# 24 instead of 16 prompt tokens take their experts by gather; the gate map is made in blocks of 8 tokens and evicted a job later

## The chip, the cores and the metric

The kernel runs on one core of a Trainium2 chip. The metric is the time of one execution in microseconds on the device; of several executions the median is taken. TensorE is called PE, VectorE DVE, ScalarE ACT, GpSimd POOL and SyncE SP, as in the profile.

## The reference

One decoder layer in fp32 for 320 tokens: 256 of a prompt and 64 of a sample (8 x 8), with a model width of 2048. The part that the change touches is the expert layer:

```
def one_block(xb):                      # after q = xb wq and two top-16 searches for each of 8 heads
    e = i1 * N_KEYS + i2                # 16 experts per token and head, of 128 * 128
    g = jax.nn.softmax(sc, axis=-1)
    ue = jnp.take(u_tab, e, axis=0)
    act = jax.nn.gelu(jnp.einsum('thkd,td->thk', ue, xb))
    ve = jnp.take(v_tab, e, axis=0)
    return jnp.einsum('thk,thkd->td', g * act, ve)
```

Before it come an input projection, windowed attention, a gating unit and an output projection; behind it a gated per-layer embedding.

## The kernel before

Up to about 400 us the kernel computes projection, attention, gating unit and output projection for all 320 tokens. Then comes the expert layer, which takes two ways.

**The dense way**, for the last 240 prompt tokens (`TD`, columns `XT:TP`): all 16,384 experts are computed. There are 128 units "u" (128 experts each: their rows `uT` times the tokens, then gelu in `finish`) and 16 groups `NG` of 8 units "v" (`v_t`, which add into `hT`). A unit's 1 MB of weights is loaded by SP in `prepare(n, 0)`; for each of its two halves `prepare(n, h)` splits it into `w_hi` (ACT, L683) and `w_lo` (DVE, L684). `multiply(n, h, q)` then does 4 chunks of three products each (`mm3`, L98 to L100: high by high, high by low, low by high), 12 for each q, 24 for a half slot (n, h). Between gelu and the v units, `weights` multiplies the activations with the gate map `g_t` and splits them too.

**The gate map** says with which weight a token takes each expert. It is made before the first v unit, in `NB` = 8 tokens at a time, 30 jobs, one behind each `multiply` of the first u units. `one_hots(j)` writes on DVE e (L762) and p (L763), where the two keys of a token's choices are marked; `map_products(j)` multiplies them on PE (L775, 16 small products into two PSUM tiles, tag "s" for even jobs and "o" for odd ones, two buffers each), evicts the two tiles on ACT into the tile `g_st` (L779), and at each second job sends `g_st`, with 16 tokens, to the DRAM tensor `gd` by a DMA on POOL's queue (L786). The pool "oh" has two buffers of `g_st`, e and p. `fetch_g` reads a group's part back, for group 0 on POOL's queue, for the others on ACT's.

**The gather way**, for the first 16 prompt tokens (`XT`) and the 64 sample tokens: their experts' rows are fetched by an indirect DMA on POOL's queue into `row`, 128 rows of 2048 at a time (a `Rows` set; "c" for the sample with 64 steps, "x" for the prompt with 16), and DVE makes a dot product (L828, first pass with rows of u) or adds the weighted rows to a sum (L832, second pass with rows of v). The indices and gates of "x" come into `x_eg` by 8 small DMAs on POOL (L737). At the end PE adds the sums of the 128 rows up by token (`add_samples` for c, L875; `add_first` for x, L907), and the results go to `hT`.

The order in the dense phase is written out by hand: `tc.manual_schedule` keeps DVE, ACT and PE to the order of the program. In the loop over the first u units each slot has its `multiply` q = 0, a map job, q = 1, a map job, and then `prepare` for the next but one half; a count of microseconds (`spent`, `total`, `step_us`) spreads the gather steps over the rest.

Two lines of the schedule matter here:

```
at_ = (2 * (slot - first) + q + 1) / (2 * (2 * U1 - first))
while job < JOBS and job < round(JOBS * at_):
```

Of the kernel before, what the change touches and what calls it, by code (L numbers as in the profile page):

```python
# [10 lines left out]
F32 = mybir.dt.float32  # L11
# [28 lines left out]
WSC = 16384.0  # L40
LEAD = 32

XT = 16
TD = TP - XT
NTB = TD // 16


def build(tc, a):
# [4 lines left out]
def _build(ctx, tc, nc, a):  # L53
# [11 lines left out]
    hl = ctx.enter_context(tc.tile_pool(name="hl", bufs=4))  # L65
    ps = ctx.enter_context(tc.tile_pool(name="ps", bufs=2, space=bass.MemoryType.PSUM))
    drm = ctx.enter_context(tc.tile_pool(name="drm", bufs=1, space=bass.MemoryType.DRAM))
    gd = drm.tile([NG, P, NTB * GRP * 16], F32, name="gd")

    def psum(tag, cols, parts=P):  # L70
        t = ps.tile([P, 512], F32, tag=tag, name="ps_" + tag)
# [450 lines left out]
    i128 = load(pr, "iota", [P, NK])  # L522
    i16 = i128[:, 0:TOPK]
    stack = load(pr, "stack", [P, TS])
    stack_x = load(pr, "stack_x", [P, XT])
    c_e = pr.tile([P, 64], I32, name="c_e")
    c_g = pr.tile([P, 64], F32, name="c_g")
    x_eg = pr.tile([P, 2, TOPK], F32, name="x_eg")
    rcol = pr.tile([P, 4], F32, name="rcol")

    c_up, up = open_pool("up")
    c_rt, rt = open_pool("rt", "right")
# [5 lines left out]

    dup = rt.tile([P, 2, TS], F32, name="dup")
    vec.tensor_copy(dup, ssq[:, TP:].unsqueeze(1).to_broadcast([P, 2, TS]))  # L540
    dup_x = rt.tile([P, PH, XT], F32, name="dup_x")
    vec.tensor_copy(dup_x, ssq[:, 0:XT].unsqueeze(1).to_broadcast([P, PH, XT]))
    pm = psum("s", 512)
    pe.matmul(pm[:, 0:TP], ones_d, ssq[:, 0:TP], start=True, stop=True)
    flat = lambda d: d.rearrange("p a b -> p (a b)")
    for i, l in enumerate((ssq[:, 0:P], ssq[:, P:TP], flat(dup), flat(dup_x))):
        pe.matmul(pm[:, TP + i : TP + i + 1], l, ones_d[:, 0:1], start=True, stop=True)
    r = rstd(rt, pm[:, 0 : TP + 4], TP + 4)
    r1 = r[:, XT:TP]
    vec.tensor_copy(rcol, r[:, TP:])  # L550

# [159 lines left out]
        del sums[n], halves[n]  # L711

    NB = 8
    JOBS = NTB * 16 // NB
    oh = {}

    def key_tables():

        f = lambda i, s: R[i][:, s].rearrange("p h k -> p (h k)")
        picks = []  # L720
        for i in range(2):
            tp = psum("tr", 384)
# [12 lines left out]
        vec.tensor_copy(ex[:, 1], R[0][:XT, 2])  # L735
        for h in range(PH):
            pool.dma_start(x_eg[h * XT : h * XT + XT], ex[:, :, h])  # L737
        return picks

    def open_tables(picks):  # L740
# [24 lines left out]

    def map_products(j):
        e, parts = oh.pop(j)
        tb, hb = divmod(j, 16 // NB)
        if hb == 0:
            oh["st"] = oh["pool"].tile([P, NK, 16], F32, name="g_st")  # L770
        for q in range(NB // 4):
            gp = psum("so"[j % 2], 512)
            for t in range(4):
                for k in range(2):
                    pe.matmul(  # L775
                        gp[:, t * P : t * P + P], e[:, 1, q, :, t], parts[:, k, q, :, t], start=k == 0, stop=k == 1
                    )
            b = hb * NB + 4 * q
            act.activation(  # L779
                oh["st"][:, :, b : b + 4].rearrange("p a t -> p t a"),  # L780
                gp.rearrange("p (t a) -> p t a", t=4),
                AF.Copy,
                scale=1.0 / WSC,
            )
        if hb == 16 // NB - 1:
            pool.dma_start(  # L786
                gd[:, :, tb * P : tb * P + P].rearrange("g p x -> p g x"),
                oh["st"].rearrange("p (g i) t -> p g (i t)", g=NG),
            )

    def rows_of(dst, tmp, sl, n):

# [42 lines left out]
                vec.tensor_mul(self.w, self.w, self.g)  # L835

    def fetch_g(g, queue=nc.scalar):
        gt = vp.tile([P, NTB, GRP, 16], F32, name="g_t")
        queue.dma_start(gt.rearrange("p a b c -> p (a b c)"), gd[g])
        return gt  # L840

    def weights(g, gt):


        groups.setdefault(g, [])
        u, w = {}, {}
        for i in range(GRP + 2):
            if i >= 2:
                vec.tensor_sub(w[i - 2][1], flat4(u[i - 2]), w[i - 2][0].bitcast(F32))  # L849
                groups[g].append(w[i - 2])  # L850
            if i < GRP:
                u[i] = acts.pop(g * GRP + i)
                m = u[i].rearrange("p (a b) -> p a b", a=NTB)
                vec.tensor_mul(m, m, gt[:, :, i])
            elif i == GRP and g + 1 < NG:
                state["g"] = fetch_g(g + 1)
            if 1 <= i <= GRP:
                k = i - 1
                if k < 4 and g < NG - 1:
                    w[k] = tails[k]  # L860
                elif k < 4:
                    if k == 0:
                        state["t"] = state["xcp"].tile([P, 8, TD], F32R, tag="xc", name="thl")
# [37 lines left out]
                yield  # L901
        vec.tensor_add(ssq, total[:, 0], total[:, 1])

    def add_first():
        pt = psum("tr", NC_ * XT)
        for c in range(NC_):
            pe.matmul(pt[:, c * XT : c * XT + XT], xx[:, c * P : c * P + P], stack_x, start=True, stop=True)  # L907
            if c % 8 == 7:
                yield
        vec.tensor_add(hT[:, :, 0:XT], hT[:, :, 0:XT], pt.rearrange("p (c t) -> p c t", c=NC_))  # L910

    state = {}
    U1 = LEAD - 4
# [17 lines left out]
    with tc.manual_schedule(engines={mybir.EngineType.DVE, mybir.EngineType.Activation, mybir.EngineType.PE}):  # L931
# [2 lines left out]
                prepare(n, h)  # L934


        steps, spent, job, first = front(), 0.0, 0, None
        for n in range(U1):
            for h in range(2):
                slot = 2 * n + h  # L940
                for q in range(2):
                    multiply(n, h, q)
                    if h == 0 and q == 0 and n:
                        finish(n - 1)
                    if first:
                        at_ = (2 * (slot - first) + q + 1) / (2 * (2 * U1 - first))
                        while job < JOBS and job < round(JOBS * at_):
                            if job + 1 < JOBS:
                                one_hots(job + 1)
                            map_products(job)  # L950
                            job += 1
                if first:
                    prepare((slot + 3) // 2, 1 - h)
                else:
                    while steps and spent < 1.4 * (slot + 1):
                        cost = next(steps, None)
                        if cost is None:
                            steps = None
                        else:
                            spent += cost  # L960
                    if steps:
                        prepare(n + 2, h)
                    else:
                        first = slot + 1
        prepare(U1 + 1, 1)
        n = U1
        shut(oh["close"])
# [3 lines left out]
        for z in (A0, C):  # L971
# [2 lines left out]
        sets = [  # L974
            Rows("c", c_e, c_g, xc, rcol[:, 2:3]),
            Rows("x", x_eg[:, 0].bitcast(I32), x_eg[:, 1], xx, rcol[:, 3:4]),
        ]
        steps = [(k, j, second) for second in (False, True) for k in sets for j in range(k.n)]
        rows = {}

        def row(m):
# [4 lines left out]

        state["g"] = fetch_g(0, pool)
        to_c = rows_of(xc, state["xd"], slice(TP, T), 2)
        to_x = rows_of(xx, state["xd"], slice(0, XT), PH)
        load = weights(0, state["g"])  # L990
        for n in range(n, LEAD):
            finish(n - 1)
# [21 lines left out]
        sums_x = None  # L1014
        last_norm = last_split()
        for n in range(LEAD, len(order)):
            finish(n - 1)
# [8 lines left out]
            for h in range(2):  # L1026
# [9 lines left out]
                if m >= len(steps) - 16:  # L1036
                    next(sums_c, None)
                if sums_x:
                    next(sums_x, None)
                if order[n][0] == "v" and order[n][1] == NG - 1 and order[n][2]:  # L1040
                    next(last_norm)
                slots += 1
                while m < len(steps) and (spent + step_us / 2 < total * slots / (2 * (END - LEAD)) or n >= END):
# [2 lines left out]
                    row(m + 3)  # L1046
                    m += 1
                    spent += step_us
                if m == len(steps) and not sums_x and n >= END:
                    sums_x = add_first()  # L1050
                if n + 2 < len(order):
                    prepare(n + 2, h)
        finish(n)
# [34 lines left out]
def _constants():  # L1088
# [32 lines left out]
    stack_x = (np.arange(P)[:, None] % XT == np.arange(XT)[None, :]).astype(np.float32)  # L1121
# [88 lines left out]
```

## Time and profile before

| | us |
|---|---|
| median of 3 runs | 2134.97 |
| lowest and highest run | 2132.25, 2137.13 |
| the profiled execution | 2136.97 |
| its span | 2135.2 |

PE is busy for 98% of the span, DVE for 80%, ACT for 47% and POOL for 15%; the mean granted clock of PE is 0.993. The span is what the trace covers; an execution's own time is 1.8 us more. In the rows below an instruction's time may overlap with its neighbour's on PE, since products are pipelined: the duration of one is no measure of how many fit into a stretch.

### The profile page before, as it was taken

Reading aid. Unit: us, or ns where it says so; the run is one execution under the profiler, and the core shown is the slowest. Engines: PE = TensorE matmul, PEld = TensorE weight load, DVE = VectorE, ACT = ScalarE, POOL = GpSimd, SP = SyncE. Lnnn points to the kernel's source line nnn. Section 1 sums busy time; section 2 is a strip of 40 time slices with the busy share of each in tenths; the row PEclk is TensorE's granted clock in tenths of the full one; section 3 lists DMA queues with packets and bytes.
Section 4 is the critical chain, followed back from the end, with each engine's and each line's share of the span. In section 5 each row is a group of like instructions: output and inputs, shape, how many; then the busy total and the mean of one; then the engine's idle time right before and its main releaser. Section 6 shows DMA issues by size and latency. Waiting matters only on the chain. (4 is left out here: it accounts for less than half of the span.)

```text
span 2135.2 us, 41032 instructions
## 1 busy us (share of the span) xinstructions
PE 2101.2 (98%) x17106; PEld 2051.5 (96%) x17106; DVE 1714.6 (80%) x2563; ACT 1002.7 (47%) x1457; POOL 315.1 (15%) x231
## 2 busy tenths in 40 slices
PE   8999999999998899999999999999999999999999
PEld 7879999999998899999999999999999999999999
DVE  6574875699997768888888898898898888885754
ACT  5346554335446665444444444444444444434632
POOL 2000000000001111222222222122222222210000
PEclk9999999999999999999999999999999999999999
DMA  7312254333556688999989999999899898884452
GB/s 280 144 62 82 101 208 165 138 139 122 183 194 188 204 317 326 379 349 351 382 352 349 361 362 351 348 376 363 334 378 359 338 375 350 333 320 170 152 181 84
DMA packets 85209, 563.06 MB, mean 264 GB/s; under 512 B 9894, under 2 KB 14438, under 8 KB 22160
## 3 DMA queue, kind: packets, MB, share of 16 engines
q1 hardware_dynamic: 49936, 349.76, 44.1%
q0 software_dynamic: 29680, 191.81, 23.6%
q10 hardware_dynamic: 5408, 18.88, 2.3%
q8 instruction: 134, 2.20, 0.4%
q14 instruction: 51, 0.42, 0.1%
HBM read 541.58 MB, written 19.79 MB: 263 GB/s over the span
## 5 line engine op out<-in xcount | busy, mean ns | idle before, releaser
L683 ACT ACTIVATE w_hi<-w_raw 128x1024 fp32r<-128x1024 f32 x512 | 542.6, 1060 | 682.7 <-PE ps_o L99 362.8
L684 DVE TENSOR_TENSOR w_lo<-w_raw,w_hi 128x1024 fp32r<-128x1024 f32 x512 | 624.6, 1221 | 206.0 <-ACT w_hi L683 204.9
L98 PE MATMUL ps_mm<-a,w_hi 128*128 128x240 f32 (+1 forms) x1776 | 518.2, 292 | 2.1 <-ACT w_hi L191 1.7
L99 PE MATMUL ps_mm<-a,w_hi 128*128 128x240 f32 (+1 forms) x1776 | 518.7, 292 | 1.0 <-DVE a L123 1.0
L100 PE MATMUL ps_mm<-a,w_lo 128*128 128x240 f32 (+1 forms) x1776 | 516.6, 291 | 2.6 <-DVE w_lo L684 2.1
L98 PE MATMUL ps_mm<-c,w_hi 128*128 128x240 f32 (+1 forms) x1280 | 362.9, 283 | 0.0
L100 PE MATMUL ps_mm<-c,w_lo 128*128 128x240 f32 (+1 forms) x1280 | 361.2, 282 | 0.0
L99 PE MATMUL ps_mm<-c,w_hi 128*128 128x240 f32 (+1 forms) x1280 | 360.9, 282 | 0.0
L99 PEld LDWEIGHTS ps_mm<-a,w_hi 128*128 128x128 f32 x1776 | 336.7, 190 | 8.9 <-issue 6.6
L98 PEld LDWEIGHTS ps_mm<-a,w_hi 128*128 128x128 f32 x1776 | 336.8, 190 | 8.4 <-issue 4.8
L100 PEld LDWEIGHTS ps_mm<-a,w_lo 128*128 128x128 f32 x1776 | 336.8, 190 | 7.0 <-issue 3.2
L81 ACT ACTIVATE w_hi<-w_raw 128x1024 fp32r<-128x1024 f32 x150 | 158.6, 1059 | 282.2 <-PE ps_mm L99 188.8
L99 PE MATMUL ps_o<-wl,w_hi 128*128 128x240 f32 x1024 | 282.0, 275 | 1.1 <-DVE wl L849 1.1
L100 PE MATMUL ps_o<-wh,w_lo 128*128 128x240 f32 x1024 | 282.3, 276 | 0.0
L98 PE MATMUL ps_o<-wh,w_hi 128*128 128x240 f32 x1024 | 278.9, 272 | 0.0
L82 DVE TENSOR_TENSOR w_lo<-w_raw,w_hi 128x1024 fp32r<-128x1024 f32 x150 | 182.5, 1220 | 94.5 <-ACT w_hi L81 91.3
L100 PEld LDWEIGHTS ps_mm<-c,w_lo 128*128 128x128 f32 x1280 | 243.4, 190 | 0.2
L98 PEld LDWEIGHTS ps_mm<-c,w_hi 128*128 128x128 f32 x1280 | 243.5, 190 | 0.0
L99 PEld LDWEIGHTS ps_mm<-c,w_hi 128*128 128x128 f32 x1280 | 243.4, 190 | 0.0
L99 PEld LDWEIGHTS ps_o<-wl,w_hi 128*128 128x128 f32 x1024 | 192.7, 188 | 1.8 <-DVE wl L849 1.7
L98 PEld LDWEIGHTS ps_o<-wh,w_hi 128*128 128x128 f32 x1024 | 194.3, 190 | 0.0
L100 PEld LDWEIGHTS ps_o<-wh,w_lo 128*128 128x128 f32 x1024 | 194.3, 190 | 0.0
(382 smaller groups left out, 3792.5 us busy)
## 6 DMA issues: line engine op xcount, KB each, us to landing
w_raw<-in_uT SPq DMA_DIRECT2D x128, 1024.0 KB, 6.3
w_raw<-in_v_t SPq DMA_DIRECT2D x128, 1024.0 KB, 8.7
w_raw<-in_w_in SPq DMA_DIRECT2D x25, 1024.0 KB, 5.0
w_raw<-in_w_out SPq DMA_DIRECT2D x16, 1024.0 KB, 4.8
w_raw<-in_wq SPq DMA_DIRECT2D x16, 1024.0 KB, 4.8
w_raw<-in_w_gate SPq DMA_DIRECT2D x16, 1024.0 KB, 5.0
gd<-g_st POOLq DMA_DIRECT2D x15, 1024.0 KB, 6.5
g_t<-gd ACTq DMA_DIRECT2D x15, 960.0 KB, 8.0
```

Source lines behind the costliest of these rows:

```text
L81: last = act.activation(hi, s, AF.Copy)
L82: (lo_eng or vec).tensor_sub(lo, s, hi.bitcast(F32))
L98: pe.matmul(out, wh, xh, start=start, stop=False)
L99: pe.matmul(out, wh, xl, start=False, stop=False)
L100: pe.matmul(out, wl, xh, start=False, stop=stop)
L683: act.activation(hi, s, AF.Copy)
L684: vec.tensor_sub(lo, s, hi.bitcast(F32))
```

## The change

- `XT` is 24, so 232 columns are dense instead of 240. The 8 new tokens form a third set "y": 8 tokens x 8 heads x 2 halves of the 16 choices, 128 rows, 8 steps in each pass. Its indices and gates come by 16 small DMAs; its tokens' rows by 16 more transposes (`rows_of`), into the buffer of "c" after that set is done; a second `add_first` sums them up, now 4 products at a time.
- The sets run one after the other, each with both passes: c, x, y instead of first passes of c and x and then second ones.
- The map is stored in 29 blocks of 8 tokens: every job has its own `g_st` and its own write to `gd`.
- Eviction and write (`map_out`) of a job are issued after the products of the next job.
- In the map stretch `prepare` stands between q = 0 and q = 1, not behind both.

```diff
-XT = 16
+XT = 24
+X1 = 16
+X2 = XT - X1
 TD = TP - XT
-NTB = TD // 16
+NTB = TD // 8
...
-    JOBS = NTB * 16 // NB
+    JOBS = NTB
...
         for h in range(PH):
-            pool.dma_start(x_eg[h * XT : h * XT + XT], ex[:, :, h])
+            pool.dma_start(x_eg[h * X1 : h * X1 + X1], ex[:X1, :, h])
+
+        for i in range(2 * PH):
+            k, h = divmod(i, PH)
+            pool.dma_start(y_eg[i * X2 : i * X2 + X2], ex[X1:, :, h, k * X2 : k * X2 + X2])
...
     def map_products(j):
         e, parts = oh.pop(j)
-        tb, hb = divmod(j, 16 // NB)
-        if hb == 0:
-            oh["st"] = oh["pool"].tile([P, NK, 16], F32, name="g_st")
+        oh["out"] = []
         for q in range(NB // 4):
             gp = psum("so"[j % 2], 512)
+            oh["out"].append(gp)
...
+    def map_out(j, out):
+        st = oh["pool"].tile([P, NK, NB], F32, name="g_st")
+        for q, gp in enumerate(out):
             act.activation(
-                oh["st"][:, :, b : b + 4].rearrange("p a t -> p t a"),
+                st[:, :, 4 * q : 4 * q + 4].rearrange("p a t -> p t a"),
...
-        if hb == 16 // NB - 1:
-            pool.dma_start(
...
+        pool.dma_start(
+            gd[:, :, j * GRP * NB : (j + 1) * GRP * NB].rearrange("g p x -> p g x"),
+            st.rearrange("p (g i) t -> p g (i t)", g=NG),
+        )
...
                             map_products(job)
+                            if out:
+                                map_out(job - 1, out)
+                            out = oh["out"]
                             job += 1
-                if first:
-                    prepare((slot + 3) // 2, 1 - h)
-                else:
+                        if q == 0:
+                            prepare((slot + 3) // 2, 1 - h)
+                if not first:
...
+        map_out(JOBS - 1, out)
         prepare(U1 + 1, 1)
...
+            Rows("y", y_eg[:, 0].bitcast(I32), y_eg[:, 1], None, rcol[:, 4:5]),
         ]
-        steps = [(k, j, second) for second in (False, True) for k in sets for j in range(k.n)]
+        steps = [(k, j, second) for k in sets for second in (False, True) for j in range(k.n)]
```

On ACT, in the middle of the map stretch (L779 is the eviction and L683 the `w_hi` of the kernel before; DMASW1 and DMASW2 are the counts of POOL's DMA queue that a write to `gd` raises, PE that of the map products), there stands before:

```order
L779 ACTIVATE g_st<-ps_o 128x4x128 [waits PE_49] x2
L683 ACTIVATE w_hi<-w_raw 128x1024 [waits DVE_49]
L779 ACTIVATE g_st<-ps_s 128x4x128 [waits DMASW1_49,PE_49,Activation_49]
L779 ACTIVATE g_st<-ps_s 128x4x128 [waits PE_49]
L779 ACTIVATE g_st<-ps_o 128x4x128 [waits PE_49] x2
L779 ACTIVATE g_st<-ps_s 128x4x128 [waits DMASW2_49,PE_49,Activation_49]
```

and in the changed kernel (L792 is the eviction, L690 the `w_hi`):

```order
L792 ACTIVATE g_st<-ps_o 128x4x128 [waits DMASW1_49,PE_49,Activation_49]
L792 ACTIVATE g_st<-ps_o 128x4x128 [waits PE_49]
L690 ACTIVATE w_hi<-w_raw 128x1024 [waits DVE_49]
L792 ACTIVATE g_st<-ps_s 128x4x128 [waits DMASW2_49,PE_49,Activation_49]
L792 ACTIVATE g_st<-ps_s 128x4x128 [waits PE_49]
L792 ACTIVATE g_st<-ps_o 128x4x128 [waits DMASW3_49,PE_49,Activation_49]
```

A wait for a write stands at the eviction of each job now, where it stood at that of each second job; it is the write of the job two places back, whose `g_st` is taken again.

On POOL's queue, from the indices of the gathers to the last of them, there stands before:

```order
L737 DMA x_eg<-ex 16x2x16 x8
L786 DMA gd<-g_st 128x16x128 x15
L839 DMA g_t<-gd 128x1920
L819 DMA row<-in_u_rows,c_e 128x2048 x64
L819 DMA row<-in_u_rows,x_eg 128x2048 x16
L819 DMA row<-in_v_rows,c_e 128x2048 x64
L819 DMA row<-in_v_rows,x_eg 128x2048 x16
```

and in the changed kernel:

```order
L744 DMA x_eg<-ex 16x2x16 x8
L748 DMA y_eg<-ex 8x2x8 x16
L798 DMA gd<-g_st 128x16x64 x29
L851 DMA g_t<-gd 128x1856
L831 DMA row<-in_u_rows,c_e 128x2048 x64
L831 DMA row<-in_v_rows,c_e 128x2048 x64
L831 DMA row<-in_u_rows,x_eg 128x2048 x16
L831 DMA row<-in_v_rows,x_eg 128x2048 x16
L831 DMA row<-in_u_rows,y_eg 128x2048 x8
L831 DMA row<-in_v_rows,y_eg 128x2048 x8
```

Sixteen small DMAs stand ahead of the first write, there are 29 writes of half the size, and 16 gathers of the set y close the row.

## Rows read from the trace of the kernel before

**Rows 1.** The page: busy time of each engine, share of the span, instructions.
```profile
PE 2101.2 (98%) x17106; PEld 2051.5 (96%) x17106; DVE 1714.6 (80%) x2563; ACT 1002.7 (47%) x1457; POOL 315.1 (15%) x231
```

**Rows 2.** Four stretches; the first line names the columns.
```profile
core 0: us, PE busy (x) PEld busy (x) DVE busy (x) ACT busy (x) POOL busy (x), PEclk, DMA share, GB/s
300.00:400.00 100.00, 100.00 (x683) 99.73 (x683) 57.11 (x78) 42.20 (x60) 8.04 (x15) 1.00 0.51 179
643.00:756.00 113.00, 100.12 (x806) 96.07 (x806) 84.45 (x72) 71.95 (x79) 16.22 (x14) 0.94 0.62 188
1000.00:1100.00 100.00, 100.00 (x897) 100.00 (x896) 89.26 (x95) 44.75 (x57) 25.17 (x15) 1.00 0.92 364
```

**Rows 3.** PE by line and form: line, tiles, shapes, count | busy us, mean ns | idle.
```profile
L98 PE MATMUL ps_mm<-c,w_hi 128*128 128x240 f32 x1024 | 283.8, 277 | 0.0
...
L100 PE MATMUL ps_o<-thl,w_lo 128*128 128x240 f32 x64 | 17.5, 274 | 0.0
```

**Rows 4.** Timeline of PE at 1942 us: start us, us, engine, line, operation, tiles.
```profile
1942.41 1.85 PE L907 MATMUL ps_tr<-c_stack_x,xx 128*128 128x16 f32 x16
```

**Rows 5.** Timeline of PE at 692 us, granted clock 0.50: first and eleventh product.
```profile
691.69 0.41 PE L99 MATMUL ps_mm<-a,w_hi 128*128 128x240 f32 x1
...
693.82 0.41 PE L100 MATMUL ps_mm<-a,w_lo 128*128 128x240 f32 x1
```

**Rows 6.** Timeline of one slot of the map stretch, all engines.
```profile
697.32 2.06 PE L775 MATMUL ps_s<-p,e 128*128 128x128 f16 x16
...
698.52 1.98 ACT L779 ACTIVATE g_st<-ps_s 128x512 f32<-128x512 f32 x2 [1.26 <-PE ps_s L775]
...
700.30 1.05 ACT L683 ACTIVATE w_hi<-w_raw 128x1024 fp32r<-128x1024 f32 x1
...
700.56 2.05 PE L775 MATMUL ps_o<-p,e 128*128 128x128 f16 x16
701.39 1.23 DVE L684 TENSOR_TENSOR w_lo<-w_raw,w_hi 128x1024 fp32r<-128x1024 f32 x1 [1.79 <-ACT w_hi L683]
701.71 2.04 ACT L779 ACTIVATE g_st<-ps_o 128x512 f32<-128x512 f32 x2 [0.35 <-PE ps_o L775]
...
703.78 1.23 DVE L763 TENSOR_TENSOR p<-e,sel 128x2048 f16<-128x2048 f16 x1
...
705.06 0.28 PE L775 MATMUL ps_s<-p,e 128*128 128x128 f16 x1 [1.11 <-DVE p L763]
```

**Rows 7.** Waits of PE from 640 to 757 us: us in total, times, longest.
```profile
PE ps_o L775 <- DVE p L763: 7.0, 7, 1.3
PE ps_s L775 <- DVE p L763: 6.2, 6, 1.1
```

**Rows 8.** Map products, writes, index transfers: ns min/median/max, first and last start us.
```profile
L775 PE MATMUL ps_s<-p,e x240: 277/297/330, 643.1 to 751.2; 128*128 128x128 f16 x120
L775 PE MATMUL ps_o<-p,e x240: 285/297/330, 646.3 to 755.7; 128*128 128x128 f16 x120
...
L786 POOL DMA_DIRECT2D gd<-g_st x15: 1152/1152/1212, 649.8 to 757.5; - x15
...
DMA to landing us min/median/max: 6.0/6.5/7.5
...
L737 POOL DMA_DIRECT2D x_eg<-ex x8: 504/507/545, 637.7 to 641.6; - x8
```

**Rows 9.** DMA issues: count, KB each, median us from issue to landing.
```profile
g_t<-gd POOLq DMA_DIRECT2D x1, 960.0 KB, 4.8
...
x_eg<-ex POOLq DMA_DIRECT2D x8, 2.0 KB, 4.1
...
c_stack_x<-in_stack_x POOLq DMA_DIRECT2D x1, 8.0 KB, 2.7
```

**Rows 10.** DVE by line and form, the set x: count | busy us, mean ns | idle.
```profile
L828 DVE SCALAR_TENSOR_TENSOR row<-row,xx 128x2048 f32<-128x2048 f32 x16 | 36.5, 2282 | 0.0
L832 DVE SCALAR_TENSOR_TENSOR xx<-row,x_w,xx 128x2048 f32<-128x2048 f32 x15 | 35.2, 2346 | 0.0
```

More of the change, by code (lines that the diff above doesn't have):

```diff
@@ L67, in _build @@
     drm = ctx.enter_context(tc.tile_pool(name="drm", bufs=1, space=bass.MemoryType.DRAM))
-    gd = drm.tile([NG, P, NTB * GRP * 16], F32, name="gd")
+    gd = drm.tile([NG, P, NTB * GRP * 8], F32, name="gd")
     def psum(tag, cols, parts=P):
@@ L524, in _build @@
     stack = load(pr, "stack", [P, TS])
-    stack_x = load(pr, "stack_x", [P, XT])
+    stack_x = load(pr, "stack_x", [P, X1])
+    stack_y = pr.tile([P, X2], F32, name="stack_y")
+    vec.tensor_add(stack_y, stack_x[:, 0:X2], stack_x[:, X2:X1])
     c_e = pr.tile([P, 64], I32, name="c_e")
@@ L528, in _build @@
     x_eg = pr.tile([P, 2, TOPK], F32, name="x_eg")
-    rcol = pr.tile([P, 4], F32, name="rcol")
+    y_eg = pr.tile([P, 2, TOPK // 2], F32, name="y_eg")
+    rcol = pr.tile([P, 5], F32, name="rcol")
     c_up, up = open_pool("up")
@@ L540, in _build @@
     vec.tensor_copy(dup, ssq[:, TP:].unsqueeze(1).to_broadcast([P, 2, TS]))
-    dup_x = rt.tile([P, PH, XT], F32, name="dup_x")
-    vec.tensor_copy(dup_x, ssq[:, 0:XT].unsqueeze(1).to_broadcast([P, PH, XT]))
+    dup_x = rt.tile([P, PH, X1], F32, name="dup_x")
+    vec.tensor_copy(dup_x, ssq[:, 0:X1].unsqueeze(1).to_broadcast([P, PH, X1]))
+    dup_y = rt.tile([P, 2 * PH, X2], F32, name="dup_y")
+    vec.tensor_copy(dup_y, ssq[:, X1:XT].unsqueeze(1).to_broadcast([P, 2 * PH, X2]))
     pm = psum("s", 512)
@@ L545, in _build @@
     flat = lambda d: d.rearrange("p a b -> p (a b)")
-    for i, l in enumerate((ssq[:, 0:P], ssq[:, P:TP], flat(dup), flat(dup_x))):
+    for i, l in enumerate((ssq[:, 0:P], ssq[:, P:TP], flat(dup), flat(dup_x), flat(dup_y))):
         pe.matmul(pm[:, TP + i : TP + i + 1], l, ones_d[:, 0:1], start=True, stop=True)
-    r = rstd(rt, pm[:, 0 : TP + 4], TP + 4)
+    r = rstd(rt, pm[:, 0 : TP + 5], TP + 5)
     r1 = r[:, XT:TP]
@@ L777, in map_products @@
                     )
-            b = hb * NB + 4 * q
+    def map_out(j, out):
+        st = oh["pool"].tile([P, NK, NB], F32, name="g_st")
+        for q, gp in enumerate(out):
             act.activation(
-                oh["st"][:, :, b : b + 4].rearrange("p a t -> p t a"),
+                st[:, :, 4 * q : 4 * q + 4].rearrange("p a t -> p t a"),
                 gp.rearrange("p (t a) -> p t a", t=4),
@@ L784, in map_products @@
             )
-        if hb == 16 // NB - 1:
-            pool.dma_start(
-                gd[:, :, tb * P : tb * P + P].rearrange("g p x -> p g x"),
-                oh["st"].rearrange("p (g i) t -> p g (i t)", g=NG),
-            )
+        pool.dma_start(
+            gd[:, :, j * GRP * NB : (j + 1) * GRP * NB].rearrange("g p x -> p g x"),
+            st.rearrange("p (g i) t -> p g (i t)", g=NG),
+        )
     def rows_of(dst, tmp, sl, n):
@@ L837, in fetch_g @@
     def fetch_g(g, queue=nc.scalar):
-        gt = vp.tile([P, NTB, GRP, 16], F32, name="g_t")
+        gt = vp.tile([P, NTB, GRP, NB], F32, name="g_t")
         queue.dma_start(gt.rearrange("p a b c -> p (a b c)"), gd[g])
@@ L862, in weights @@
                     if k == 0:
-                        state["t"] = state["xcp"].tile([P, 8, TD], F32R, tag="xc", name="thl")
+                        state["t"] = state["xcp"].tile([P, 8, TD], F32R, tag="xx", name="thl")
                     w[k] = [flat4(state["t"][:, j]) for j in (2 * k, 2 * k + 1)]
@@ L902, in last_split, with add_first @@
         vec.tensor_add(ssq, total[:, 0], total[:, 1])
-    def add_first():
-        pt = psum("tr", NC_ * XT)
+    def add_first(x, sums, t0, n):
+        pt = psum("tr", NC_ * n)
         for c in range(NC_):
-            pe.matmul(pt[:, c * XT : c * XT + XT], xx[:, c * P : c * P + P], stack_x, start=True, stop=True)
-            if c % 8 == 7:
+            pe.matmul(pt[:, c * n : c * n + n], x[:, c * P : c * P + P], sums, start=True, stop=True)
+            if c % 4 == 3:
                 yield
-        vec.tensor_add(hT[:, :, 0:XT], hT[:, :, 0:XT], pt.rearrange("p (c t) -> p c t", c=NC_))
+        vec.tensor_add(hT[:, :, t0 : t0 + n], hT[:, :, t0 : t0 + n], pt.rearrange("p (c t) -> p c t", c=NC_))
     state = {}
@@ L934, in _build @@
                 prepare(n, h)
-        steps, spent, job, first = front(), 0.0, 0, None
+        steps, spent, job, first, out = front(), 0.0, 0, None, None
         for n in range(U1):
@@ L988, in _build @@
         to_c = rows_of(xc, state["xd"], slice(TP, T), 2)
-        to_x = rows_of(xx, state["xd"], slice(0, XT), PH)
+        to_x = rows_of(xx, state["xd"], slice(0, X1), PH)
         load = weights(0, state["g"])
@@ L1013, in _build @@
         sums_c = add_samples()
-        sums_x = None
+        sums_x = sums_y = None
         last_norm = last_split()
@@ L1035, in _build @@
                         spent += 0.8 if at_ <= GRP else 0.0
-                if m >= len(steps) - 16:
-                    next(sums_c, None)
+                if m >= 2 * sets[0].n and sums_c and next(sums_c, "end") == "end":
+                    sums_c = None
+                    sets[2].x = state["xcp"].tile([P, D], F32, tag="xc", name="xy")
+                    to_x = rows_of(sets[2].x, state["xd"], slice(X1, XT), 2 * PH)
                 if sums_x:
                     next(sums_x, None)
+                if sums_y:
+                    next(sums_y, None)
                 if order[n][0] == "v" and order[n][1] == NG - 1 and order[n][2]:
@@ L1048, in _build @@
                     spent += step_us
-                if m == len(steps) and not sums_x and n >= END:
-                    sums_x = add_first()
+                if m >= len(steps) - 2 * sets[2].n and not sums_x:
+                    sums_x = add_first(xx, stack_x, 0, X1)
+                if m == len(steps) and not sums_y:
+                    sums_y = add_first(sets[2].x, stack_y, X1, X2)
                 if n + 2 < len(order):
@@ L1120, in _constants @@
     stack = (np.arange(P)[:, None] % TS == np.arange(TS)[None, :]).astype(np.float32)
-    stack_x = (np.arange(P)[:, None] % XT == np.arange(XT)[None, :]).astype(np.float32)
+    stack_x = (np.arange(P)[:, None] % X1 == np.arange(X1)[None, :]).astype(np.float32)
     iota = np.broadcast_to(np.arange(P, dtype=np.float32), (P, P))
```

## The prediction

> **What bounds the kernel now.** I read the busy shares first: PE is busy for 2101.2 of 2135.2 us [rows 1], so the span is the sum of what PE has to do, and an edit gains only by shortening PE's work or one of its few waits. The second view was the table by stretches: in the dense expert phase (stretches at 1000 us) PE is busy for all 100 us, beside a vector engine at 89 us and a DMA share of 0.92; in the map stretch it is busy for 100 of 113 us, at a mean granted clock of 0.94 [rows 2]. So two questions remain: what one dense product costs PE, and where PE waits at all. PE's gaps lie in one place, the map stretch, where the gate map is made between dense U products: PE waits 13 times there for the one-hots p, 7.0 + 6.2 us in all [rows 7].
>
> **What a dense product costs.** The dense phase has 12,288 of them (nine groups of 1024, six of 480, three of 64; the first and the last are shown), each of 240 moving columns behind a weight load of 128 columns [rows 3]. The mean of 277 ns in these rows is a pipeline's latency, not its rate; the rate is the count in a stretch: 100 us / 897 = 111.5 ns at 240 columns, 100 us / 683 = 146.4 ns at 320 columns [rows 2]. Two other rows say what sets the 111.5. Products of only 16 columns run 16 in 1.85 us, or some 0.11 us each [rows 4]. And where the granted clock is 0.50 (that is 1.2 GHz), ten products of 240 columns start 2.13 us apart, 213 ns each [rows 5]; a cost of the columns alone would be 240 / 1.2 = 200 ns. A product of 16 columns that costs as much as one of 240 is not bound by columns but by what both share, the load of 128 weight columns. At 320 columns the columns bind (146.4 ns), at 240 the load does.
>
> **Narrowing, 240 to 232 columns: 0.** If columns bound it, the slope between the two stretches, (146.4 - 111.5) / 80 = 0.44 ns for one column, would give 8 x 0.44 x 12,288 = 43 us. On the reading above it gives nothing, and I take nothing. The Trainium skill ("TensorE: Matmul & The Clock Gate", section "Back-to-back issue gap") puts a product at N / 2.4 + 2.5 ns, which is 102.5 ns for 240 columns and 99.2 for 232, an estimated gain of 41 us; its section "LDWEIGHTS (loading the stationary operand)" puts a load of 128 columns at 106.7 ns. The trace's 111.5 lies above both and nearer to the second, and by that rule the load hides the whole gain.
>
> **The map stretch: 0.** Before, it runs from 643.1 us to 755.7 + 0.3 = 756.0 us, with 30 jobs of 8 tokens [rows 8]. A job is 16 small products and 12 dense ones; two jobs without a wait start 700.56 - 697.32 = 3.24 us apart, with the wait 705.06 - 700.56 = 4.50 us, so two take 7.74 us [rows 6]. 29 x 3.24 + 2.05 = 96.0 us would be free of waits; the other 16.9 us are the 13.2 us of waits and some 4 us at half clock [rows 5, 7]. The wait is a chain on ACT and DVE: eviction of a job (1.98 us), behind it w_hi (1.05), w_lo (1.23), then e and p (1.23 each, e has the same form), then the map products [rows 6]. The change cuts it: an eviction is issued one job later, where its products are long done, and w_hi moves between the two halves of a slot, so that neither holds w_lo, e and p.
>
> But it adds a wait. Each job now has its own tile g_st, of which there are still two, and its own write by the POOL queue: 29 writes of 512 KB in pieces of 256 B, for 15 of 1 MB in pieces of 512 B. By the order of ACT, the eviction of job j+2 waits for the write of job j. Behind that eviction on ACT stand w_hi and the next eviction; behind those DVE's w_lo, and PE, which wants the PSUM tile of the job (each of the two tags holds one job). Before, the same wait came once in four jobs. So two jobs take at least 2.04 (an eviction, [rows 6]) + 0.30 (release and start, an estimate from the 0.35 us that ACT idles behind PE in [rows 6]) + L, with L the time from issue to landing of a write.
>
> A write of 1 MB takes 6.5 us in the middle (6.0 to 7.5) [rows 8]. Its fixed part is about 2.7 us, what a transfer of 8 KB takes [rows 9], so 3.8 us are data. L for half the bytes in the same number of pieces (128 x 16): if bytes cost, 2.7 + 1.9 = 4.6; if pieces cost, 6.5 as now; if a short piece costs twice, 2.7 + 7.6 = 10.3. Row-wise transfers of the same size are faster (960 KB in 4.8 us, [rows 9]), that is 2.1 us of data against 3.8, so pieces of 512 B do already pay something by the piece: (3.8 - 2.1) + 2.1 / 2 = 2.75, L = 5.5. This I take.
>
> The start is also later. The eviction of the second job waits for every DMA that was queued on POOL before it, and the change puts 16 small y_eg transfers behind the 8 x_eg ones. Those start at 637.7 to 641.6 us [rows 8], 0.56 us apart, so the 24th starts at 637.7 + 23 x 0.56 = 650.5 and lands 4.1 us later [rows 9], at 654.6. From there the eviction of job 25 is 12 periods away, and behind it come its own 2.0 us, w_hi 1.05, the eviction of job 26 with 2.0, and the last map with 2.05 plus 0.3 of hand-over: end = 654.6 + 12 x (2.34 + L) + 7.4 = 690.1 + 12 L. With L = 5.5 that is 756.1, against 756.0: one job fewer and the cut chain pay for the new wait, no more.
>
> **What else PE gets: +5.5.** A third set y (8 tokens x 8 heads x 2 halves) needs 16 more transposes, 1.8 us at 0.11, and its sum over rows is 16 products that run as 32 passes, as 8 of the old sum run as 16 [rows 4], 3.6 us; one more column of the norm adds 0.1. All of it is in PE's full stretch, so it counts whole.
>
> **g_t(0): +1.** The first read of the map is queued on POOL behind the last write; 960 KB land in 4.8 us [rows 9]. The last eviction waits for a write that did not exist before, so it is 0 to 2 us later. I take 1.
>
> **16 more gathers: 0.** y adds 16 gathers of 1 MB and 16 vector steps of 2.28 or 2.35 us [rows 10], 37 us. DVE idles 10.7 of 100 us in the dense phase [rows 2], 117 us over the 1090 us in which the steps are spread; 16.8 MB are 42 us of DMA time at 364 / 0.92 = 396 GB/s, against 8% of 1090 = 87 us idle. Both fit, on average. If that cover is gone (steps bunch, and a weight half comes late), a quarter to a half of the 42 us shows, 10 to 21 us. The steps' new order (both passes of a set together) and the doubled yields of the sums move work inside PE's full stretch and cost 0.
>
> **Sum.** 2136.97 (the profiled execution; its span is 2135.2) + 0 + 0.1 + 5.5 + 1 = 2143.6. The median of the runs lies 2.0 below that execution, at 2134.97, so the forecast is 2141.6, rounded to 2142.
>
> **The rivals.** *A fast write (the other side).* If L is under 4.95, the stretch shortens by more than the 6.5 us that PE gains, and the kernel is faster; 4.6 gives 690.1 + 55.2 = 745.3, so 2134.97 - 10.7 + 6.5 = 2131; with no wait for writes at all the end is 643.1 + 28 x 3.24 + 2.05 = 735.9, so 2121. For it: the DMA share of the map stretch is 0.62, against 0.92 later [rows 2], so a write finds free engines. Against: it needs pieces to cost by bytes alone, which the 4.8 and 6.5 us speak against. *A slow write.* L of 6.5 gives 768.1, so 2154; L of 10.3 gives 813.7, so 2199. For it: the piece halves while their number stays. The Trainium skill ("DMA: Bandwidth & Descriptors", section "Specifications") asks for 512 B or more for line rate, with a read-modify-write below that; no run here yet has 256 B writes of this size. *Width pays after all*: 2142 - 43 = 2099; against it stand the products of 16 columns and the 213 ns. *Gathers overload DVE or DMA*: 2152 to 2163; against it, no wait of PE shows in the dense phase.
>
> **How the numbers follow.** Forecast, L from 4.95 to 6: 0.42. Fast write: 0.20. Slow write: 0.26. Width: 0.06. Gathers: 0.06. The median of the likeliest is 2142. About 0.2%, or 4.3 us, is what a measurement of this kernel tells from no change: 2130.7 to 2139.2, which is L from 4.6 to 5.3. So faster is width with 0.06 and the lower part of the fast writes with 0.14; same is the rest of these with 0.06 and the forecast's lower part with 0.18; slower is the forecast's rest with 0.24, slow writes and gathers: 0.56. The range reaches from L = 4.2 (2126) to L = 6.8 (2157) and a gather cost of 16 us: 2126 to 2158. It leaves out width, the very slow write and writes that never bind.
>
> **What would show it.** Count of dense products in 100 us after 1000: still 897, not 920. The write's landing: 5.5 us; ACT's evictions waiting for DMA, PE's map products waiting for ACT where they waited for DVE, two jobs 7.8 us apart, and the last map product at 756. In the dense phase no wait of PE for w_lo. The prediction is wrong if the map stretch ends before 745 or after 768, if the count rises, or if waits for w_lo appear between 800 and 1950 us.

## The result and the profile after

| | before | changed |
|---|---|---|
| median, us | 2136.72 | 2153.52 |
| lowest and highest of 5 runs | 2132.25, 2138.84 | 2150.51, 2155.06 |
| the profiled execution | 2136.97 | 2154.34 |
| its span | 2135.2 | 2152.6 |

The ratio is 1.0078 with a 95% interval of 1.0064 to 1.0092: the changed kernel is 16.8 us slower. The forecast was slower, at 2142 in a range of 2126 to 2158; the size came out at more than twice the 7 us that were added up.

The stretches of the changed kernel, with columns as in [rows 2], here the first 100 us after 100, the map stretch twice (the frame of [rows 2], then a wider one), and two of the dense phase:

```profile
100.00:200.00 100.00, 99.49 (x663) 81.95 (x662) 66.42 (x170) 53.06 (x173) 0.55 (x1) 0.95 0.18 64
643.00:756.00 113.00, 97.44 (x762) 94.29 (x761) 82.45 (x70) 67.77 (x72) 39.99 (x45) 0.89 0.69 180
640.00:770.00 130.00, 110.50 (x866) 107.11 (x864) 90.58 (x79) 78.99 (x86) 46.14 (x53) 0.89 0.70 184
1000.00:1100.00 100.00, 100.00 (x896) 100.00 (x895) 91.15 (x104) 45.60 (x60) 25.21 (x16) 1.00 0.91 360
1700.00:1800.00 100.00, 100.00 (x896) 100.00 (x895) 89.51 (x94) 46.76 (x63) 25.39 (x15) 1.00 0.93 356
```

and of the kernel before, the same early stretch and the wider map frame:

```profile
100.00:200.00 100.00, 99.50 (x673) 82.15 (x672) 66.56 (x170) 53.78 (x174) 0.54 (x1) 0.97 0.19 66
...
640.00:770.00 130.00, 116.58 (x939) 112.44 (x939) 93.46 (x79) 83.10 (x98) 22.95 (x24) 0.93 0.66 205
```

Two things are to be seen. The dense phase runs at 896 products in 100 us, as before with 897: 232 columns cost what 240 do. Of the signs that the prediction named for the dense phase, a wait of PE for w_lo between 800 and 1950 us did not appear; PE waited 1.3 us there in all, for wl. And the map stretch got fewer products through (762 in 113 us for 806 in [rows 2]), with less busy time and a lower mean clock.

Where the 17.4 us of the two spans lie is read from the timelines, at the instruction that closes each unit (its gelu, or its addition to hT). The difference between the same unit's ends, changed less before:

| stretch | difference grows by, us |
|---|---|
| start to the first u unit (532 us) | +2.2 |
| first to the twentieth unit (641 us) | 0.0 |
| map stretch and the 20 us behind it (to 790 us) | +7.8 |
| dense phase to 1586 us | +1.0 |
| 1586 to 2000 us (set y, sums) | +6.9 |
| the rest | -0.5 |

The first row belongs to no edit: in the early stretch above the granted clock was 0.95 for 0.97, with the same work. The profiled execution of a_last, which is shown below and does the same work up to there at a granted clock of 1.00, ends its first unit 4.8 us earlier than this one.

PE's waits in the map stretch (us in total, times, longest) answer to [rows 7]:

```profile
PE ps_s L785 <- DVE p L774: 5.8, 6, 1.3
PE ps_o L785 <- DVE p L774: 4.2, 2, 2.1
PE ps_o L785 <- ACT g_st L792: 4.0, 3, 1.9
PE ps_tr L810 <- ACT xd L813: 3.9, 1, 3.9
PE ps_s L785 <- ACT g_st L792: 1.6, 2, 1.1
```

and ACT's own, in the same stretch:

```profile
ACT g_st L792 <- DMA gd<-g_st: 38.6, 23, 3.0
ACT g_st L792 <- DMA y_eg<-ex: 7.3, 1, 7.3
```

where the kernel before had these:

```profile
ACT g_st L779 <- PE ps_s L775: 21.0, 10, 2.7
ACT g_st L779 <- PE ps_o L775: 18.4, 12, 2.4
```

In the kernel before, ACT's evictions waited above all for PE's map products; now ACT stands 38.6 us for writes of the map, 23 times. PE still waits 10.0 us for p, and 5.6 us more of a new kind, for the evictions themselves. The writes and map products themselves, in the columns of [rows 8]:

```profile
L785 PE MATMUL ps_s<-p,e x240: 276/297/330, 645.3 to 760.7; 128*128 128x128 f16 x120
...
L798 POOL DMA_DIRECT2D gd<-g_st x29: 1152/1152/1218, 654.7 to 766.6; - x29
...
DMA to landing us min/median/max: 4.8/4.9/8.2
```

A write of 512 KB lands after 4.9 us in the middle, faster than the 5.5 that was assumed. Yet the last map product starts at 760.7 us. The timeline of ACT and POOL shows how a write holds an eviction: first the issues of two writes on POOL, then ACT's row at the beginning, in the middle and at the end of the stretch:

```profile
658.27 1.17 POOL L798 DMA_DIRECT2D gd<-g_st  x1 [2.30 <-ACT g_st L792]
...
720.79 1.15 POOL L798 DMA_DIRECT2D gd<-g_st  x1 [1.80 <-ACT g_st L792]
```

```profile
655.92 2.05 ACT L792 ACTIVATE g_st<-ps_o 128x512 f32<-128x512 f32 x2 [7.29 <-DMA y_eg<-ex]
657.74 1.09 ACT L690 ACTIVATE w_hi<-w_raw 128x1024 fp32r<-128x1024 f32 x1
659.71 2.10 ACT L792 ACTIVATE g_st<-ps_s 128x512 f32<-128x512 f32 x2 [0.88 <-DMA gd<-g_st]
...
663.20 2.12 ACT L792 ACTIVATE g_st<-ps_o 128x512 f32<-128x512 f32 x2 [1.19 <-DMA gd<-g_st]
...
718.23 2.16 ACT L792 ACTIVATE g_st<-ps_o 128x512 f32<-128x512 f32 x2
...
729.08 2.08 ACT L792 ACTIVATE g_st<-ps_o 128x512 f32<-128x512 f32 x2 [2.70 <-DMA gd<-g_st]
...
752.17 2.13 ACT L792 ACTIVATE g_st<-ps_o 128x512 f32<-128x512 f32 x2 [0.52 <-DMA gd<-g_st]
...
764.17 2.00 ACT L792 ACTIVATE g_st<-ps_s 128x512 f32<-128x512 f32 x2 [0.62 <-DMA gd<-g_st]
765.96 1.06 ACT L690 ACTIVATE w_hi<-w_raw 128x1024 fp32r<-128x1024 f32 x1
...
767.16 0.69 ACT L813 ACTIVATE xd<-hT,c_gains 128x128 f32<-128x128 f32 x2
```

The eviction of an odd job ends at 657.97, its write is issued 0.30 us later, and the eviction that takes the same tile again begins at 663.20, which is 658.27 + 4.9. That period, from one eviction of an odd job to the next, is 7.28 us. But from 655.92 to 752.17 there are 12 such periods, 8.02 us each in the mean. The longest is that from 718.23 to 729.08, 10.85 us, where the write issued at 720.79 held the tile for 8.3 us. At the end, w_hi and the transposes' inputs xd come only behind the last eviction.

### The profile page after: what moved, and what is told of

The parts are those of the page before. It is cut to its first block, busy times and chain, and to the rows that moved or that the text cites. A ratio compares the mean times of both kernels' runs of the same rounds, so it can differ in the third digit from the quotient of the medians.

```text
span 2152.6 us, 41236 instructions
## 1 busy us (share of the span) xinstructions
PE 2110.8 (98%) x17140; PEld 2061.1 (96%) x17140; DVE 1740.1 (81%) x2589; ACT 1008.5 (47%) x1476; POOL 365.7 (17%) x277
## 5 line engine op out<-in xcount | busy, mean ns | idle before, releaser
L690 ACT ACTIVATE w_hi<-w_raw 128x1024 fp32r<-128x1024 f32 x512 | 543.1, 1061 | 674.6 <-PE ps_o L101 317.0
L100 PE MATMUL ps_mm<-a,w_hi 128*128 128x232 f32 (+1 forms) x1776 | 521.3, 294 | 1.3 <-ACT w_hi L193 1.0
L101 PE MATMUL ps_mm<-a,w_hi 128*128 128x232 f32 (+1 forms) x1776 | 520.8, 293 | 1.2 <-DVE a L125 1.2
L102 PE MATMUL ps_mm<-a,w_lo 128*128 128x232 f32 (+1 forms) x1776 | 519.0, 292 | 2.6 <-DVE w_lo L691 2.1
L100 PE MATMUL ps_mm<-c,w_hi 128*128 128x232 f32 (+1 forms) x1280 | 364.9, 285 | 0.0
L102 PE MATMUL ps_mm<-c,w_lo 128*128 128x232 f32 (+1 forms) x1280 | 362.5, 283 | 0.0
L101 PE MATMUL ps_mm<-c,w_hi 128*128 128x232 f32 (+1 forms) x1280 | 362.1, 283 | 0.0
L101 PEld LDWEIGHTS ps_mm<-a,w_hi 128*128 128x128 f32 x1776 | 340.4, 192 | 9.2 <-issue 6.6
L100 PEld LDWEIGHTS ps_mm<-a,w_hi 128*128 128x128 f32 x1776 | 340.7, 192 | 7.6 <-issue 4.8
L101 PE MATMUL ps_o<-wl,w_hi 128*128 128x232 f32 x1024 | 282.8, 276 | 2.2 <-DVE wl L861 2.1
L100 PE MATMUL ps_o<-wh,w_hi 128*128 128x232 f32 x1024 | 280.4, 274 | 0.0
L102 PE MATMUL ps_o<-wh,w_lo 128*128 128x232 f32 x1024 | 279.3, 273 | 0.0
L100 PEld LDWEIGHTS ps_mm<-c,w_hi 128*128 128x128 f32 x1280 | 246.6, 193 | 0.0
L101 PEld LDWEIGHTS ps_mm<-c,w_hi 128*128 128x128 f32 x1280 | 246.4, 192 | 0.0
```

Source lines behind the costliest of these rows:

```text
L100: pe.matmul(out, wh, xh, start=start, stop=False)
L101: pe.matmul(out, wh, xl, start=False, stop=False)
L102: pe.matmul(out, wl, xh, start=False, stop=stop)
L690: act.activation(hi, s, AF.Copy)
```

## The experiments

The theory was that the second wait of the sum, an eviction that waits for the write two jobs back with two tiles g_st, makes the loss in the map stretch, that the 8 columns save nothing, and that the set y costs PE what its instructions take. Against it stood that the short pieces load the DMA engines until these are the bound, that the later eviction itself holds up w_hi, and that columns do count. All ratios are to the kernel before, run on the same chip.

### Four tiles g_st

```diff
-        st = oh["pool"].tile([P, NK, NB], F32, name="g_st")
+        st = oh["pool"].tile([P, NK, NB], F32, name="g_st", bufs=4)
```

> The changed kernel with four tiles g_st instead of two; nothing else differs. Theory (the wait for a write two jobs back costs the time): ACT's 38.6 us of waits for writes go but for a few us, the last map product starts near 742 instead of 760.7, the last eviction no longer holds the next w_hi (4 to 5 us), so 2153.5 - 18 - 5 = 2130, between 2126 and 2138. Rival (writes in pieces of 256 B load the DMA engines so that they are the bound): four tiles only queue more writes, landings grow, and the time stays at 2148 to 2154. Rival (the later eviction itself holds up w_hi): 2150 to 2154 too, with the waits of PE for p as they are.

Measured: 2128.12 us, ratio 0.9961 (0.9947 to 0.9974), 25.4 us under the changed kernel by the medians. PE's waits and the wider map frame:

```profile
PE ps_o L785 <- ACT g_st L792: 2.3, 1, 2.3
PE ps_tr L810 <- ACT xd L813: 2.1, 3, 1.0
PE ps_s L785 <- DVE p L774: 1.4, 2, 0.8
```

```profile
640.00:770.00 130.00, 124.03 (x1061) 121.46 (x1060) 104.54 (x100) 98.66 (x125) 48.78 (x53) 0.99 0.87 258
```

```profile
L785 PE MATMUL ps_s<-p,e x240: 277/297/303, 642.2 to 737.7; 128*128 128x128 f16 x120
```

The last map product starts at 737.7 us. With two more tiles PE's waits fall from some 20 us to 6, and the mean clock rises from 0.89 to 0.99, with the same short pieces and the same late evictions. Both rivals fall: the wait for the write makes the loss, and the DMA engines, though the short pieces do load them more (see the last section), carry them at a share of 0.87 and are not the bound.

### The later eviction with the moved split, on the kernel before

```diff
...
                             map_products(job)
+                            if out:
+                                map_out(job - 1, out)
+                            out = oh["out"]
                             job += 1
-                if first:
-                    prepare((slot + 3) // 2, 1 - h)
-                else:
+                        if q == 0:
+                            prepare((slot + 3) // 2, 1 - h)
+                if not first:
...
         prepare(U1 + 1, 1)
+        map_out(JOBS - 1, out)
```

(`map_out` holds the eviction and the write of each second job, moved out of `map_products`.)

> The kernel before (16 tokens, 240 columns, writes of 16 tokens) with only two parts of the change: evictions and writes issued one job later, and the split of the next weight half placed between q = 0 and q = 1. Theory: PE's 13.2 us of waits for p and part of the 4 us at half clock go, since the eviction of a second job alone waits for a write four jobs back: 2136.7 - 13 to 17 = 2120 to 2124. Rival (the later eviction itself costs): 2137 to 2145.

Measured: 2121.36 us, ratio 0.9930 (0.9916 to 0.9943).

```profile
PE ps_tr L803 <- ACT xd L806: 2.8, 2, 2.3
PE ps_o L774 <- DVE p L763: 0.8, 1, 0.8
PE ps_s L774 <- DVE p L763: 0.7, 1, 0.7
PE ps_o L774 <- ACT g_st L784: 0.6, 1, 0.6
```

The 13.2 us of waits for p in [rows 7] are 1.5. So the change holds a part worth 15 us, and the rest of it takes twice that back. The later eviction without the moved split was not run.

### The moved split alone

```diff
-                if first:
-                    prepare((slot + 3) // 2, 1 - h)
-                else:
+                        if q == 0:
+                            prepare((slot + 3) // 2, 1 - h)
+                if not first:
```

> The kernel before with the split of the next weight half placed between q = 0 and q = 1 of the map slots, and evictions where they were. Theory (the chain from an eviction over w_hi and w_lo to p is what PE waits for; w_hi still stands behind the eviction of the job just made): about half of b_defer's gain, 2126 to 2134. Rival (the place of the split alone makes the gain, the later eviction none): 2121. Other rival: 2136 or more, the gain is all in the later eviction.

Measured: 2139.03 us, ratio 1.0012 (1.0002 to 1.0021). PE's waits:

```profile
PE ps_o L775 <- DVE p L763: 9.3, 8, 2.4
PE ps_s L775 <- DVE p L763: 5.1, 5, 1.1
```

They are as long as before, 14.4 us for 13.2. The expectation of half the gain was a miss, and the rival that named 2136 or more came true: w_hi still stands on ACT behind an eviction that waits for its products (34.3 us for PE in this stretch). The moved split gives nothing without the later eviction; whether the later eviction needs the moved split stays open.

### Blocks of 8 tokens alone

```diff
...
-        if hb == 0:
-            oh["st"] = oh["pool"].tile([P, NK, 16], F32, name="g_st")
+        oh["st"] = oh["pool"].tile([P, NK, NB], F32, name="g_st")
...
-        if hb == 16 // NB - 1:
-            pool.dma_start(
...
+        pool.dma_start(
+            gd[:, :, j * GRP * NB : (j + 1) * GRP * NB].rearrange("g p x -> p g x"),
```

> The kernel before with only the blocks of 8 tokens: each job has its own g_st and its own write of 512 KB in pieces of 256 B; evictions stay where they were. Theory (the wait for the write counts, a write lands in 4.9 us): two jobs take at least 2.05 + 0.3 + 4.9 = 7.3 us, near the 7.7 us that they take anyway, so 2136.7 to 2148. Rival (short pieces load the DMA engines): 2150 or more, landings over 6.5 us.

Measured: 2144.67 us, ratio 1.0039 (1.0024 to 1.0054); a write lands after 5.1 us in the middle.

```profile
PE ps_s L773 <- DVE p L763: 10.5, 8, 3.2
PE ps_o L773 <- DVE p L763: 8.0, 7, 2.1
```

```profile
ACT g_st L777 <- DMA gd<-g_st: 30.1, 17, 4.7
```

The write for each job costs 8 us by itself: ACT waits 30.1 us for writes, and PE 18.5 us for p behind that.

### Products 48 columns narrower

The products behind the first chunk of each sum leave out the last 48 columns of a unit u (12 of each 58 of a unit v).

```diff
-                mm3(pt, w, x[:, 0], x[:, 1], h == 0 and c == 0, h == 1 and c == 7)
+                k = TD if h == 0 and c == 0 else 184
+                mm3(pt[:, 0:k], w, x[:, 0, 0:k], x[:, 1, 0:k], h == 0 and c == 0, h == 1 and c == 7)
...
```

> The changed kernel with 11,136 of its 12,288 dense products cut from 232 to 184 columns (the products behind the first chunk of a sum leave out the last 48 columns of a unit u, and 12 of each 58 of a unit v); the rest is the same. Theory (the load of 128 weight columns sets 111.5 ns): no change, 2150 to 2156, 896 products in 100 us. Rival (columns count, 0.44 ns each): 11,136 x 48 x 0.44 ns = 235 us less, 1918.

Measured, in a single execution: 2156.92 us, against 2153.52 for the changed kernel (2150.51 to 2155.06), and just above the 2150 to 2156 expected. The group of such products and a stretch of them:

```profile
L100 PE MATMUL ps_mm<-c,w_hi 128*128 128x184 f32 x1024 | 285.0, 278 | 0.0
```

```profile
800.00:1000.00 200.00, 200.00 (x1796) 200.00 (x1795) 178.24 (x195) 93.76 (x124) 51.65 (x31) 1.00 0.94 367
```

1796 products in 200 us are 111.4 ns each, most of them at 184 columns; the changed kernel has 1788 there at 232. So 235 us that columns would have given are not there. By the starts of the products between 840 and 1580 us, those of the u units lie 111.7 ns apart at 240 columns (before), at 232 (changed) and at 184 alike; those of the v units lie 112.0, 112.2 and 111.8 ns apart. From 184 to 240 columns a product's cost moves by less than 0.5 ns.

### The last eviction behind the split

```diff
-        map_out(JOBS - 1, out)
         prepare(U1 + 1, 1)
+        map_out(JOBS - 1, out)
```

> The changed kernel with the eviction and write of the last job issued behind the split of the next weight half (prepare) instead of ahead of it; two tiles g_st as in the change. Theory (the last eviction waits for a write and holds w_hi and w_lo, PE idles 3.9 us before the transposes and runs at half clock behind that): 2153.5 - 4 to 5 = 2149. Rival (PE waits there for other work, the transposes' inputs behind the same eviction): no change, 2153.

Measured: 2152.69 us, ratio 1.0081 (1.0063 to 1.0099), no different from the changed kernel. The timeline of ACT behind the map shows why:

```profile
756.80 2.17 ACT L792 ACTIVATE g_st<-ps_o 128x512 f32<-128x512 f32 x2 [1.61 <-DMA gd<-g_st]
758.76 1.06 ACT L690 ACTIVATE w_hi<-w_raw 128x1024 fp32r<-128x1024 f32 x1
759.75 2.02 ACT L792 ACTIVATE g_st<-ps_s 128x512 f32<-128x512 f32 x2
...
761.86 0.67 ACT L813 ACTIVATE xd<-hT,c_gains 128x128 f32<-128x128 f32 x2
```

w_hi comes ahead now, but the inputs xd of the transposes still stand behind the last eviction, and PE waits for them (6.1 us in 4 times). The rival was right: two things stand behind that eviction, and one was moved.

### All but the set y and the 232 columns

This is the kernel before with the later eviction, the moved split, one write for each job of 8 tokens and four tiles g_st. Against a_gst4 it lacks the set y and the 232 columns, and it keeps the old order of the sets too.

```diff
...
+    def map_out(j, out):
+        st = oh["pool"].tile([P, NK, NB], F32, name="g_st", bufs=4)
...
```

> The kernel before with the later eviction, the moved split, blocks of 8 tokens with one write for each job, and four tiles g_st: all of a_gst4 but the third set of gathers and the 232 columns. Theory (the set y costs PE 5.5 us and its 16 index transfers hold the first evictions, columns give nothing): 2128.1 - 5.5 - 1 to 3 = 2119 to 2122, as b_defer. Rival (the 8 columns do save PE time, hidden in a_gst4 by the set y): 2128 or more.

Measured: 2118.07 us, ratio 0.9922 (0.9908 to 0.9935), 10.0 us under a_gst4. So with the same edits to the map stretch 24 tokens, with their order of the sets, are slower than 16. The spans of the two profiled executions differ by 2124.7 - 2115.0 = 9.7 us. By the ends of the units, 1.5 of these lie ahead of the first u unit, where the two programs do nearly the same, 1.4 in the dense phase to 1586 us and 6.9 from there to 1990 us.

### The index transfers on another queue

```diff
-            pool.dma_start(y_eg[i * X2 : i * X2 + X2], ...)
+            nc.sync.dma_start(y_eg[i * X2 : i * X2 + X2], ...)
```

(in a_gst4)

> a_gst4 with the 16 index transfers of the set y on SP's queue instead of POOL's, so that they run beside the 8 of the set x. Theory (they hold ACT's second eviction for 7.7 us, and PE waits 2.3 us for it, with a stretch of half clock or a late w_lo behind): 2128.1 - 2 to 4 = 2125. Rival (the 7.7 us of ACT are hidden, or the weight load queued behind them on SP comes late instead): 2128 or more.

Measured: 2126.45 us, ratio 0.9950 (0.9938 to 0.9963), beside 0.9961 of a_gst4; the intervals overlap, and this stays undecided. ACT waited 5.8 us for these transfers instead of 7.7 us.

### The later start of the v units' operands

```diff
-                if 2 * (n - U1) + h >= 4:
-                    for _ in range(3):
+                if 2 * (n - U1) + h >= 5:
+                    for _ in range(4):
```

On the later eviction alone (b_defer):

> b_defer with the first steps of making the v units' operands issued one half slot later (from the sixth half slot of the last four u units, four steps each, instead of from the fifth, three each). In b_defer DVE and ACT stand 3.5 us at the first read of the map, with w_hi behind them, and PE idles 2.5 us. Theory: that stand-still goes, 2121.4 - 2 to 4 = 2118. Rival: the same steps come in a bunch just before the first v unit and PE waits there instead: 2121.

On the kernel with blocks of 8 and four tiles (b_defer8):

> b_defer8 (16 tokens, later eviction, one write for each job, four tiles g_st) with the later start of the v units' operands of b_best. Theory (both shorten what stands behind the last map products: the smaller last write lands earlier, and DVE and ACT stand less at the first read): 2118.1 - 1 to 4 = 2115. Rival (with the smaller writes the first read is no longer waited for, so the later start only bunches the steps): 2118 or more.

Measured: 2116.66 us, ratio 0.9914 (0.9901 to 0.9928), and 2116.22 us, ratio 0.9902 (0.9888 to 0.9915). The second is the fastest kernel here, 20 us under the one before. For both, the interval overlaps that of the kernel it builds on (0.9916 to 0.9943 for b_defer, 0.9908 to 0.9935 for b_defer8), so that the later start's own gain is not told clearly from none. In its map stretch little is left:

```profile
640.00:770.00 130.00, 127.81 (x1109) 125.61 (x1109) 108.82 (x105) 104.60 (x129) 40.66 (x36) 1.00 0.90 268
```

and PE's waits there:

```profile
PE ps_tr L799 <- ACT xd L802: 1.5, 2, 1.2
PE ps_s L774 <- DVE p L763: 0.7, 1, 0.7
```

1109 products in the frame, for 939 before and 866 in the changed kernel, at full clock.

## Why the prediction was right, and where not

The forecast had the direction and its range held the time, but not for the reasons that it gave. Its sum was 0 for the map stretch, 1 behind it, 5.5 for the set y; the profiles show 2.8, 5.0 and 6.9, with 1.0 of drift in the dense phase, 2.2 ahead of the first unit that is no effect of the change, and -0.5 at the end: 17.4 instead of 6.6.

**Width: right.** 896 products in 100 us for 897, and 48 columns less made no difference.

**The cut chain: right.** The later eviction takes PE's waits for p away (b_defer), worth 14.8 us by the medians (2136.19 on the same chip, less 2121.36); the prediction had 16.9 us of waits and half clock to give back. For the split's new place no share in it is shown: by itself it gave nothing (b_move).

**The new wait: right in kind, wrong in size.** This is the step that failed. L was taken as 5.5 and measured 4.9, which by the prediction's own end, 690.1 + 12 L, gives 748.9 and would have made the kernel about as fast as before (2134.97 - 7.1 + 6.6 = 2134.5). So it was luck that the forecast came out slower: a landing taken 0.6 us too long, 7 us in 12 periods, stood in for a period taken too short, 10 us at the end of the map. The last map group in fact ended near 761.0, or 758.8 without the 2.2 us that lay ahead of it. The error is in the period: 2.34 + L is the least that two jobs can take, and it was used as what they do take. It was 8.02 us. Of the 9.4 us by which the 12 periods exceed 12 x (2.34 + 4.9), 3.6 lie in the one period with the slow write; writes came to land after up to 8.2 us. For the rest the rows allow this reading, which no run isolates: the evictions of odd and even jobs stand in one row on ACT, so that a wait of either kind holds the other, and with it w_hi, and 8 of PE's 14 waits were followed by products at half clock. The rival of the fast writes (L under 4.95: faster) had its condition met, and the kernel was slower; the rival of the slow ones had the time, 2154, and not the cause.

**The clock.** The prediction put half clock at some 4 us in the kernel before, and nothing of it into the end of the changed stretch, which it took from the chain of writes alone. By the starts of the products between 640 and 775 us, PE lost this much:

| kernel | waits over 0.5 us, sum in us | dense products at 213 ns | their excess over 111.5 ns, us |
|---|---|---|---|
| before | 15.3 | 56 | 5.7 |
| changed | 21.6 | 85 | 8.7 |
| b_blk8 | 21.6 | 69 | 7.0 |
| b_defer | 5.7 | 24 | 2.4 |
| a_gst4 | 6.6 | 10 | 1.0 |
| b_all | 2.7 | 0 | 0.0 |

6.3 us more of waits and 3.0 us more at half clock, less the 2.05 us of a job that is gone, are 7.2 of the 7.8 us that the map stretch and what follows it cost.

**Behind the map: mis-sized.** +1 was put down for the first read of g_t. PE lost 5 us more there than before: 3.9 us of wait for xd, behind ACT's last eviction, and 21 products at half clock for 15. The prediction named w_hi behind an eviction, but not what else stands in ACT's row when the map is over. The first read itself was never waited for in the changed kernel.

**The set y: 5.5 forecast, 6.9 measured between 1586 and 2000 us.** 16 transposes and 32 passes are in the trace (48 transposes for 32, and one more sum of 32 passes); 1.0 us more is PE's wait for wl (2.1 us in 3 times, 1.1 in 2 before). What the other 0.4 is was not tried. The 1 us by which the dense phase drifts ahead of 1586 us lies in the products of the v units: 0.26 ns more for each of some 3,900; why they are slower at 232 columns stays open. PE waits there for no gather and no w_lo, so the cover of the 16 gathers held.

## What to carry to other kernels

A wait that is cut is worth what stands there next: count the tiles of a rotating buffer against the time of the transfer that frees them, before an eviction is moved or a write is halved; here two more tiles turned 16.8 us lost into 8 us gained. A sum over in-order queues needs the period that the shared queue gives to both chains, not the least time of one chain. And before columns are saved, divide the length of a full stretch by the number of its products: if products of 16 columns cost as much as those of 240, narrower ones gain nothing, and what the moved tokens cost on the other way comes on top.

## What the runs showed of the hardware

A write to DRAM of 512 KB in pieces of 256 B landed after 4.9 us in the middle, one of 1 MB in pieces of 512 B after 6.5 us: nearer to the 4.6 us that the prediction worked out for a cost by bytes than to the 6.5 for a cost by pieces. But the short pieces did load the DMA engines more. This is POOL's queue from 643 to 756 us (packets, MB moved, share of the 16 engines' time), which carries the map's writes and little else, in b_defer with pieces of 512 B and in b_defer8 with pieces of 256 B:

```profile
q0 software_dynamic: 4386, 17.93, 50.0%
...
q0 software_dynamic: 4659, 18.18, 63.9%
```

For each MB the engines were busy 26% longer; between the kernel before (14.68 MB at 46.7%) and b_blk8 (14.12 MB at 53.8%) it is 20%. The Trainium skill ("DMA: Bandwidth & Descriptors", section "Specifications") asks for 512 B for line rate; these rows agree that pieces of 256 B cost more, though in the engines' time and hardly in the landing.

When the map ran faster, landings of the same writes grew: 5.4 us in a_gst4 and 6.3 us in b_defer8, at a DMA share of 0.87 and 0.89 in the wider map frame.

In the frame of the table above, PE's granted clock fell to 0.50 (1.2 GHz) behind 5 of 13 waits in the kernel before and behind 8 of 14 in the changed one, and 5 to 21 dense products then ran at 213 ns in place of 111.5. So the waits of this stretch cost more than a third as much again (15.3 and 5.7 us before, 21.6 and 8.7 in the changed kernel). Not every wait does: in b_all, with three gaps of 0.6 to 1.5 us between products, no product ran at half clock.
